# Stacked attention scores: the keys' low parts in both halves of the rows

## The chip, the cores and the metric

The kernel runs on one core of one Trainium2 chip. The metric is the device time of one execution in microseconds (us). Five engines work side by side, each in the order of its own queue: TensorE (PE in the profile; its weight loads have a row of their own, PEld), VectorE (DVE), ScalarE (ACT), GpSimd (POOL) and SyncE (SP, which issues most of the DMAs).

## The reference

Two stacks of two layers each work on 512 tokens of 1024 features in float32. A layer of the first stack projects the normalised tokens, runs three attention mixers beside each other, adds their projected results under sigmoid gates, and ends in a SwiGLU. The second stack has a retention layer and a gated linear recurrence. The change touches two of the three mixers of the first stack. Both have heads of 64 features:

```python
# dilated mixer, three groups of four heads; a group's band of keys per block of 128 queries
s = jnp.einsum('ncqhd,nckhd->nchqk', qb, kb) * (D ** -0.5)   # D = 64
s = jnp.where(mask, s, NEG_INF)                              # then softmax, then P V
# neighbourhood mixer, eight heads; each query sees 8 x 16 keys of the 8 x 64 grid
s = jnp.einsum('bchd,bcnhd->bhcn', q_row, kg) * scale + bias # then softmax, then P V
```

## The kernel before

**Precision.** TensorE reads float32r, which holds fewer bits than float32. Every operand is therefore kept as a pair: `split` (lines 267 to 274) writes the high part on ACT (`hi = round(src)`) and the low part on DVE (`lo = src - hi`). A product of two pairs is three matmuls, high x high, high x low and low x high (`mm3`, lines 283 to 285), all added into one PSUM bank.

**Stacked scores.** A head of 64 features fills half of TensorE's 128 rows. For group 0 of the dilated mixer and for the neighbourhood mixer the kernel therefore stacks the parts. A slot of the pool `R` is a tile [128, 2, 512]; the two heads of a pair (`e` = 0, 1) use its two halves of 512 columns. `stack_q` puts a query's high part into the 64 rows of its own side and the low part into the other 64. `stack_k` puts the keys' high part into both sides of one slot, and the keys' low part into the own side only of a second slot. `stacked` then needs two matmuls instead of three:

```python
SIDES = ((slice(0, 64), slice(64, 128)), (slice(64, 128), slice(0, 64)))
nc.tensor.matmul(s, lhsT=q[:, e, qsl], rhs=k[0][:, e, ksl], start=True, stop=False)       # line 750, 128 rows
nc.tensor.matmul(s, lhsT=q[own, e, qsl], rhs=k[1][own, 0, ksl], start=False, stop=True)   # line 751, 64 rows
```

The stationary operand is a block of 128 queries, the moving one the keys: 512 of them in the dilated mixer (32 calls over the two layers), 192 or 256 in the neighbourhood mixer (32 calls each). The dilated mixer's other groups (`s1`) and all other products go through `mm3` or `pv`. `pv` (lines 714 and 715) multiplies one stationary block of values, high parts and low parts beside each other, with the high and then with the low parts of the transposed softmax. The first mixer (MLA) has scores of 96 rows, through `mm3`.

**Order of the work.** The three mixers follow one another in each layer: MLA, dilated, neighbourhood. In each, `pipeline` issues the scores of a block one or two blocks ahead of the rest of it (softmax on DVE and ACT, transposes on PE by lines 903, 1051, 1056 and 1170, splits, `pv`). Between the blocks lie projections of the next pair (`chunk`, 24 matmuls of `mm3` each), among them those that end in `stack_q` and `stack_k`, and the merges of the mixer before (`fill`). Semaphores, and the order of instructions on each engine, are set when the program is built, by a planner that follows the program's order as a priority and starts what it holds to be ready. `high_priority` moves the splits of weights forward. `stack_k` runs twelve times: in each of the two layers for two pairs of heads of dilated group 0 and four pairs of the neighbourhood mixer.

Of the kernel before, what the change touches and what calls it, by code (L numbers as in the profile page):

```python
# [24 lines left out]
WPRI = 120  # how far ahead of the program's order weight splits are placed  # L25
HPRI = 400  # the same for the splits of h
LD = (3, 2)  # of every LD[0] LRU weight units, LD[1] go through R's slots
NG = 5  # tiles of the first branch's gates made before the attention
PD = (2, 2, 1)  # depth of the attention pipelines: MLA, dilated, neighbourhood
NM = (4, 2, 4, 1, 4, 2)  # per mixer: of every NM[2i] blocks, NM[2i+1] scale the softmax by the row sum on ACT  # L30


# ---------------------------------------------------------------- host layout
# Token order of the first block: (column group of 8, row, column in the group) of the 8 x 64 grid.
# [4 lines left out]
def _shape_constants():  # L39
# [13 lines left out]
    # dilated attention: position (b, i) is token NA_TOK[4 i + b]  # L53
# [32 lines left out]
def _na_bias_index():  # L86
    """For each query block: index into one head's flat rpb table, or one past it where no key is seen."""
    out = []
    n = 15 * 31
    for qb, (kb0, off, w) in enumerate(NA_Q):  # L90
        qt = NA_TOK[qb * 128:(qb + 1) * 128]
        k0 = kb0 * 128 + off if qb else 0
        kt = NA_TOK[k0:k0 + w]
        qr, qc = qt // 64, qt % 64
        kr, kc = kt // 64, kt % 64
        cs = np.clip(qc - 8, 0, 48)
        seen = (kc[None] >= cs[:, None]) & (kc[None] < cs[:, None] + 16)
        idx = (kr[None] - qr[:, None] + 7) * 31 + (kc[None] - qc[:, None] + 15)
        out.append(np.where(seen, idx, n))
    return np.concatenate(out, 1)  # L100
# [7 lines left out]
def _tiles(w):  # L108
    """[K, N] -> [N/128, 128, K/128, 128]: one output tile's weights lie together per partition."""
    k, n = w.shape  # L110
    return w.reshape(k // 128, 128, n // 128, 128).transpose(2, 1, 0, 3)


def _wide(w):
    """[K, 512] -> [K/256, 128, 2, 4, 128]: four output tiles' weights, two row tiles to a unit."""
    k, n = w.shape
    return w.reshape(k // 256, 2, 128, n // 128, 128).transpose(0, 2, 1, 3, 4)
# [21 lines left out]
def layout(inp):  # L139
# [32 lines left out]
    # [l, unit, 128, chunk, k tile, 128]  # L172
# [41 lines left out]
# ---------------------------------------------------------------- the kernel  # L214
# [12 lines left out]
def kernel(ctx: ExitStack, tc: tile.TileContext, d, out):  # L227
# [35 lines left out]
    # ---- primitives  # L263
# [3 lines left out]
    def split(src, hi, lo, scale=None):  # L267
        """src = hi + lo exactly, both on the float32r grid (scale: a number or a column)."""
        if scale is None:
            nc.scalar.copy(out=hi, in_=src)  # L270
            nc.vector.tensor_tensor(out=lo, in0=src, in1=f(hi), op=ALU.subtract)  # L271
        else:
            nc.scalar.activation(out=hi, in_=src, func=AF.Copy, scale=scale)
            nc.vector.scalar_tensor_tensor(out=lo, in0=src, scalar=scale, in1=f(hi), op0=ALU.mult, op1=ALU.subtract)
# [15 lines left out]
    def wload(src, n, keep=False):  # L290
        """A unit of weights from DRAM as a pair; kept in general slots, or in the ring until the unit after next."""
# [17 lines left out]
    def proj(ps, ap, n, rhs, keep=False):  # L309
        """ps = W^T x: W's tiles [128, n, 128] in DRAM, rhs the (hi, lo) pairs of x's n tiles.  # L310

        keep: the weights go through general slots, for more of them on their way."""
# [12 lines left out]
    def wide(pss, ap, n, rhs, ahead=(), norm=None):  # L325
        """Four output tiles at once, a row tile of x after another: for an x that is still being made.

        ahead: the first units' weights, where they are on their way; norm: x's, finished on the way."""
# [12 lines left out]
    def out_proj(first, rest, n, rhs, sink):  # L341
        """Eight output tiles, the first four of them wide."""
        pss = [MB.get() for _ in range(4)]
        wide(pss, first, n, rhs)
        for m in range(4):
            sink(m, pss[m])
            MB.put(pss[m])
        for m in range(4, 8):
            ps = MB.get()
            proj(ps, rest[m - 4], n, rhs)  # L350
            sink(m, ps)
            MB.put(ps)

    class Norm:
        """1 / sqrt(mean square over the features + eps): a column per block of tokens, and a row on all partitions."""
# [15 lines left out]
        def means(self, n, bank=None):  # L371
# [16 lines left out]
            # one Newton step, past the square root's table  # L388
# [16 lines left out]
    def warm_sqrt(dep):  # L405
        """The square root's table, loaded ahead of the norm that follows dep."""
# [7 lines left out]
    # ---- swiglu  # L414
    def ffn(h, norm, l4, later=None, between=()):
        """silu(x W1) (x W3): norm scales x where h doesn't hold that yet; later makes h's second half of the tokens."""
# [54 lines left out]
    # ---- tokens on the partitions: output projections with the norms behind them  # L471
    def half(ap, hf, nat):
        """Columns of half the tokens of a tile, with the tokens in their own order or in the first block's."""
# [4 lines left out]
    def wide_halves(pss, ap, rhs, later, nat):  # L478
        """As wide, for x's eight tiles: half of the tokens, and then (later makes them) the others."""
# [13 lines left out]
    def rstd(sm):  # L493
        """sm[:, 4] = 1 / sqrt((sm[:, 0] + sm[:, 1]) / D + eps)"""
# [16 lines left out]
    def out_tokens(src, n, act, gain, nxt, xt=None):  # L511
        """x (in FX, by blocks of tokens) += rms(y W) gain, or x = rms(xt + y W) gain; y's n tiles are act.

        nxt None: x goes out. Else it is the column of the next norm's gain: returns the next h, with its first half of
        the tokens made, and what makes the second. Ahead of a mixer the tokens go back to their own order."""
# [66 lines left out]
        def turn(hf):  # L582
            """Half the tokens of h, with the features back on the partitions."""
# [38 lines left out]
    # ---- the first block's mixers  # L622
    def first_layer(l, xsrc, h, norm, ahead=()):
# [28 lines left out]
        def merge(i, y, wname, m0, early):  # L652
            """merged += (1 + tanh(gate / 2)) (y W) for two tiles; the gate's first branch was made early, in place."""
# [25 lines left out]
        def pipeline(blocks, ahead):  # L679
            """blocks: (before, scores, rest); scores go out some blocks ahead of the rest."""  # L680
# [11 lines left out]
        def soft(pt, sm, src, negmax, ri, scalar):  # L692
            """pt = exp(src - max) / sum over the keys; the scaling on ScalarE or on VectorE."""
# [10 lines left out]
        # Values lie by (token block, head): 64 columns of the high parts and 64 of the low ones, so that a product  # L704
        # with P^T holds the two sums in the two halves of its rows.
        def value_split(ps, v, b0, nb, scale=None):
            """ps [128 tokens, nb blocks x 4 heads x 64] into blocks b0.. of v's two slots."""
# [9 lines left out]
        def pv_sum(o, rows):  # L717
            """A head's sums: the two halves of o's rows together, in the given rows."""
# [12 lines left out]
        # Queries and keys of 64 rows, of two heads: a query's high and low parts lie in the two halves of the rows,  # L731
        # against the keys' high parts twice; then its high parts against the keys' low ones.
# [8 lines left out]
        def stack_k(z):  # L741
            hi, lo = R.get(), R.get()
            for e, (own, other) in enumerate(SIDES):
                split(z[own], hi[own, e], lo[own, 0])
                nc.scalar.copy(out=hi[other, e], in_=z[own])
            return hi, lo

        def stacked(s, e, q, qsl, k, ksl):
            own = SIDES[e][0]
            nc.tensor.matmul(s, lhsT=q[:, e, qsl], rhs=k[0][:, e, ksl], start=True, stop=False)  # L750
            nc.tensor.matmul(s, lhsT=q[own, e, qsl], rhs=k[1][own, 0, ksl], start=False, stop=True)  # L751

        # ---------------- multi-head latent attention
# [183 lines left out]
        # ---------------- dilated attention, positions (b, i) = token 4 i + b of the stored order  # L937
# [7 lines left out]
        def vproj(g, order4):  # L945
            """Token-major values of four heads: [128 tokens, 4 blocks, 256] as (hi, lo) slots."""
# [148 lines left out]
        # ---------------- neighbourhood attention  # L1095
# [28 lines left out]
        def na_block(p, e, qb):  # L1124
# [36 lines left out]
            def rest():  # L1161
# [9 lines left out]
                # slot of (key block, query) in this half: key blocks hf .. hf + 2, two query blocks each  # L1171
# [10 lines left out]
                # key block, first column of its slots, first output column, width  # L1182
# [32 lines left out]
        # ---------------- output projection and residual  # L1215
# [27 lines left out]
    # ---------------- first block  # L1243
    nc.vector.memset(f(ones), 1.0)
    nc.vector.memset(epsc, EPS)
    # the tensor engine's clock rises while the first loads are on their way
# [53 lines left out]
    # ---------------- second block: x is kept with the tokens on the partitions, in the first block's order  # L1300
# [6 lines left out]
    def mixed(z, own):  # L1307
        """A mixer's output tile as a pair, with the tokens in the first block's order."""
# [7 lines left out]
    # ---------------- retention  # L1316
# [11 lines left out]
    for hd in range(4):  # L1328
# [21 lines left out]
        # values, token-major  # L1350
# [80 lines left out]
    # ---------------- gated linear recurrence  # L1431
    hp = [pair(t) for t in h]
    # cs = -8 softplus(-a) = -8 (max(-a, 0) + log1p(exp(-|a|))), log1p(e) = 2 atanh(e / (2 + e)) by its series
# [17 lines left out]
    # half the gate biases, for sigmoid(z) = (1 + tanh(z / 2)) / 2  # L1451
# [9 lines left out]
    for n in range(6):  # L1461
# [47 lines left out]
        for i in range(2):  # L1509
# [3 lines left out]
            # mult^2 = -expm1(2 log a) = T (1 + a^2), T = tanh(-log a)  # L1513
# [42 lines left out]
```

## Time and profile before

| | before |
|---|---|
| device time, median of 3 runs | 3357.36 us (3356.54 to 3357.69) |
| profiled execution, span from its first to its last instruction | 3360.7 us |
| PE busy | 3329.5 us, 99% |
| DVE busy | 1812.8 us, 54% |
| ACT busy | 1439.7 us, 43% |
| mean DMA rate | 93 GB/s |

Busy means that an instruction of the engine is in progress; the ends of matmuls are modelled, and consecutive matmuls overlap in the records. The pace of PE is therefore read from the starts: the time from one matmul's start to the next one's. For the profiled execution no time beside its span is on record; the span is 3.3 us (0.1%) above the median of the runs.

### The profile page before, as it was taken

What the parts mean: (1) busy time and instruction counts of PE and PEld (TensorE: products, weight loads), DVE (VectorE), ACT (ScalarE), POOL (GpSimd) and SP (SyncE); (2) the same over time, 40 slices, a digit from 0 to 9 for tenths busy, and PEclk for the clock granted to TensorE, in tenths of its full rate; (3) what the DMA queues carried; (4) which work ended last, traced back from release to release, by engine and by line L of the source; (5) the groups of instructions that cost most, each with busy time, mean ns of one, the idle gap of its engine ahead of it and who ended that gap; (6) DMA issues with size and microseconds to landing.
All of it is one profiled execution on the core that took longest, in us unless ns stands there. A gap on an engine that the chain in (4) does not pass through costs nothing.

```text
span 3360.7 us, 40433 instructions
## 1 busy us (share of the span) xinstructions
PE 3329.5 (99%) x15970; PEld 2798.7 (83%) x15970; DVE 1812.8 (54%) x3018; ACT 1439.7 (43%) x2321; POOL 125.3 (4%) x127
## 2 busy tenths in 40 slices
PE   9999999999999999999999999999999999999999
PEld 7898888888888898888888888888888888788887
DVE  7837765555347738765444355554433257753323
ACT  5735653432236626653332234433422247742322
POOL 0000001011000000001011000000000000000000
PEclk9999999999999999999999999999999999999999
DMA  4113323322333113223223322223133332223232
GB/s 160 52 49 97 94 75 101 114 96 94 102 121 95 51 60 105 91 67 125 94 94 110 126 76 85 85 79 113 63 97 104 107 107 94 80 84 101 94 104 90
DMA packets 97439, 313.77 MB, mean 93 GB/s; under 512 B 12000, under 2 KB 16736, under 8 KB 97248
## 3 DMA queue, kind: packets, MB, share of 16 engines
q1 hardware_dynamic: 95376, 308.33, 28.8%
q8 instruction: 125, 2.05, 0.3%
q10 hardware_dynamic: 1872, 2.85, 0.2%
q14 instruction: 66, 0.54, 0.0%
HBM read 298.55 MB, written 4.19 MB: 90 GB/s over the span
## 4 chain that ended last, share of the span: by engine, by line
PE 91%; ACT 4%; DVE 3%; DMA 1%; issue 1%; POOL 0%; DVEq 0%; ACTq 0%; SPq 0%
PE b L283 28%; PE b L285 28%; PE b L284 28%; PE b L715 1%; PE b L714 1%; PE b L751 1%; DVE wlo L271 1%; ACT r L270 1%; DVE fa L277 1%; PE b L1170 1%; PE b L903 1%; ACT whi L270 1%; DVE r L271 1%; DMA raw<-in_gu_dram 0%; PE b L750 0%
## 5 line engine op out<-in xcount | busy, mean ns | idle before, releaser
L283 PE MATMUL b<-r,whi 128*128 128x512 f32 (+1 forms) x3032 | 1168.3, 389 | 10.1 <-ACT whi L270 3.7
L284 PE MATMUL b<-r,whi 128*128 128x512 f32 (+1 forms) x3032 | 1170.6, 387 | 0.0
L285 PE MATMUL b<-r,wlo 128*128 128x512 f32 (+1 forms) x3032 | 1161.5, 387 | 0.0
L270 ACT CAST whi<-raw 128x1024 fp32r<-128x1024 f32 (+2 forms) x486 | 506.7, 1043 | 1231.2 <-PE b L284 696.3
L271 DVE TENSOR_TENSOR wlo<-raw,whi 128x1024 fp32r<-128x1024 f32 (+2 forms) x486 | 632.8, 1302 | 635.9 <-ACT whi L270 628.8
L283 PEld LDWEIGHTS b<-r,whi 128*128 128x128 f32 x3032 | 567.6, 188 | 126.4 <-ACT whi L270 5.5
L285 PEld LDWEIGHTS b<-r,wlo 128*128 128x128 f32 x3032 | 570.5, 188 | 114.1 <-issue 1.0
L284 PEld LDWEIGHTS b<-r,whi 128*128 128x128 f32 x3032 | 571.1, 188 | 111.2 <-issue 0.5
L284 PE MATMUL b<-wlo,r 128*128 128x512 f32 (+1 forms) x1040 | 393.6, 378 | 0.5 <-DVE wlo L271 0.5
L285 PE MATMUL b<-whi,r 128*128 128x512 f32 (+1 forms) x1040 | 393.3, 378 | 0.0
L283 PE MATMUL b<-whi,r 128*128 128x512 f32 (+1 forms) x1040 | 322.4, 377 | 1.4 <-ACT whi L270 1.4
L283 PEld LDWEIGHTS b<-whi,r 128*128 128x128 f32 x1040 | 222.3, 214 | 30.4 <-ACT whi L270 2.3
L284 PEld LDWEIGHTS b<-wlo,r 128*128 128x128 f32 x1040 | 222.4, 214 | 30.1 <-issue 1.0
L285 PEld LDWEIGHTS b<-whi,r 128*128 128x128 f32 x1040 | 222.5, 214 | 29.0 <-issue 1.0
L283 PE MATMUL b<-r,r 128*128 128x512 f32 (+4 forms) x640 | 226.8, 357 | 6.2 <-ACT p L694 5.4
L284 PE MATMUL b<-r,r 128*128 128x512 f32 (+4 forms) x640 | 225.2, 353 | 0.1
L285 PE MATMUL b<-r,r 128*128 128x512 f32 (+4 forms) x640 | 223.9, 352 | 0.0
L277 DVE TENSOR_TENSOR fm<-b,fa 128x512 f32<-128x512 f32 x120 | 82.7, 691 | 238.8 <-PE b L285 238.7
L270 ACT CAST r<-b 128x512 fp32r<-128x512 f32 (+3 forms) x264 | 125.8, 495 | 117.3 <-PE b L1170 29.4
L277 DVE TENSOR_TENSOR fa<-fa,fa 128x512 f32<-128x512 f32 x202 | 135.6, 696 | 63.3 <-ACT fa L1392 29.0
L271 DVE TENSOR_TENSOR r<-b,r 128x512 fp32r<-128x512 f32 (+3 forms) x264 | 147.1, 570 | 37.7 <-ACT r L270 36.7
L277 DVE TENSOR_TENSOR fm<-b,fm 128x512 f32<-128x512 f32 (+2 forms) x86 | 59.1, 687 | 175.9 <-PE b L285 135.3
(167 smaller groups left out, 2937.3 us busy)
## 6 DMA issues: line engine op xcount, KB each, us to landing
raw<-in_gu_dram SPq DMA_DIRECT2D x176, 512.0 KB, 3.5
raw<-in_w_in_dram SPq DMA_DIRECT2D x96, 512.0 KB, 3.6
raw<-in_f_out_dram SPq DMA_DIRECT2D x44, 512.0 KB, 3.5
raw<-in_r_in_dram SPq DMA_DIRECT2D x32, 512.0 KB, 3.5
raw<-in_l_in_dram SPq DMA_DIRECT2D x24, 512.0 KB, 3.5
raw<-in_w_tok_dram SPq DMA_DIRECT2D x22, 512.0 KB, 3.5
raw<-in_w_v_dram SPq DMA_DIRECT2D x20, 512.0 KB, 3.9
raw<-in_r_v_dram SPq DMA_DIRECT2D x16, 512.0 KB, 3.9
```

The source lines that it names most:

```text
L270: nc.scalar.copy(out=hi, in_=src)
L271: nc.vector.tensor_tensor(out=lo, in0=src, in1=f(hi), op=ALU.subtract)
L277: nc.vector.tensor_tensor(out=out_, in0=a, in1=b, op=op)
L283: nc.tensor.matmul(ps, lhsT=l[0], rhs=r[0], start=start, stop=False)
L284: nc.tensor.matmul(ps, lhsT=l[0], rhs=r[1], start=False, stop=False)
L285: nc.tensor.matmul(ps, lhsT=l[1], rhs=r[0], start=False, stop=stop)
L714: nc.tensor.matmul(o, lhsT=lt, rhs=ph, start=start, stop=False)
L715: nc.tensor.matmul(o, lhsT=lt, rhs=pl, start=False, stop=stop)
L751: nc.tensor.matmul(s, lhsT=q[own, e, qsl], rhs=k[1][own, 0, ksl], start=False, stop=True)
L903: nc.tensor.transpose(tp[:, k * 128:k * 128 + 128], b["p"][:, k * 128:k * 128 + 128], ident)
L1170: nc.tensor.transpose(t0[:, k * 128:k * 128 + 128], pt[:, k * 128:k * 128 + 128], ident)
```

## The change

Three lines of code are edited, and comments and docstrings are replaced by empty lines or dropped, with the line numbers kept (one line more in `stack_k`, one less in `stacked`; the two matmuls stay lines 750 and 751). The keys' low part of head `e` now lies in half `e` of the slot's columns (before, both heads' low parts lay in half 0, in different rows), and an ACT copy puts it into the other 64 rows as well. The second matmul takes all 128 rows of the stacked queries, the same stationary operand as the first. It so adds low x low to the scores, which before were left out. No slot is added: the second slot of `stack_k` was a whole tile before.

```diff
         def stack_k(z):
             hi, lo = R.get(), R.get()
             for e, (own, other) in enumerate(SIDES):
-                split(z[own], hi[own, e], lo[own, 0])
+                split(z[own], hi[own, e], lo[own, e])
                 nc.scalar.copy(out=hi[other, e], in_=z[own])
+                nc.scalar.copy(out=lo[other, e], in_=f(lo[own, e]))
             return hi, lo

         def stacked(s, e, q, qsl, k, ksl):
-            own = SIDES[e][0]
             nc.tensor.matmul(s, lhsT=q[:, e, qsl], rhs=k[0][:, e, ksl], start=True, stop=False)
-            nc.tensor.matmul(s, lhsT=q[own, e, qsl], rhs=k[1][own, 0, ksl], start=False, stop=True)
+            nc.tensor.matmul(s, lhsT=q[:, e, qsl], rhs=k[1][:, e, ksl], start=False, stop=True)
```

## Rows read from the trace of the kernel before

**Rows 1.** The page: busy time by engine, and the chain that ended last.

```profile
PE 3329.5 (99%) x15970; PEld 2798.7 (83%) x15970; DVE 1812.8 (54%) x3018; ACT 1439.7 (43%) x2321; POOL 125.3 (4%) x127
...
PE 91%; ACT 4%; DVE 3%; DMA 1%; issue 1%; POOL 0%; DVEq 0%; ACTq 0%; SPq 0%
```

**Rows 2.** PE's waits, 248 to 530 us: total, times, longest (us).

```profile
PE b L750 <- DVE sm L1153: 0.6, 1, 0.6
```

**Rows 3.** Line 751, whole run: duration ns min/median/max, first and last start, shapes.

```profile
L751 PE MATMUL b<-r,r x96: 351/381/502, 248.4 to 1490.4; 64*128 64x512 f32 x32, 64*128 64x256 f32 x32, 64*128 64x192 f32 x32
```

**Rows 4.** Timeline of PE, first dilated block: start us, duration us.

```profile
247.85 0.39 PE L285 MATMUL b<-r,wlo 128*128 128x512 f32 x1
248.08 0.39 PE L750 MATMUL b<-r,r 128*128 128x512 f32 x1
248.40 0.50 PE L751 MATMUL b<-r,r 64*128 64x512 f32 x1
248.83 0.38 PE L283 MATMUL b<-r,r 128*128 128x256 f32 x1
249.05 0.28 PE L284 MATMUL b<-r,r 128*128 128x256 f32 x1
```

**Rows 5.** Timeline of the weight loads there, idle time in brackets.

```profile
248.40 0.18 PEld L751 LDWEIGHTS b<-r,r 64*128 64x128 f32 x1 [0.35 <-issue]
248.82 0.19 PEld L283 LDWEIGHTS b<-r,r 128*128 128x128 f32 x1 [0.25 <-issue]
```

**Rows 6.** Timeline of PE, neighbourhood blocks of 192 and of 256 keys.

```profile
388.39 0.25 PE L750 MATMUL b<-r,r 128*128 128x192 f32 x1
388.58 0.35 PE L751 MATMUL b<-r,r 64*128 64x192 f32 x1
388.86 0.50 PE L285 MATMUL b<-r,wlo 128*128 128x512 f32 x1
389.20 0.40 PE L283 MATMUL b<-r,whi 128*128 128x512 f32 x1
...
389.89 0.28 PE L750 MATMUL b<-r,r 128*128 128x256 f32 x1
390.09 0.38 PE L751 MATMUL b<-r,r 64*128 64x256 f32 x1
390.40 0.39 PE L715 MATMUL b<-r,r 128*128 128x256 f32 x1
390.63 0.28 PE L714 MATMUL b<-r,r 128*128 128x256 f32 x1
390.74 0.27 PE L715 MATMUL b<-r,r 128*128 128x256 f32 x1
```

**Rows 7.** Timeline of PE, MLA scores of 96 rows.

```profile
146.41 0.40 PE L283 MATMUL b<-r,r 96*128 96x512 f32 x1
146.64 0.40 PE L284 MATMUL b<-r,r 96*128 96x512 f32 x1
146.88 0.39 PE L285 MATMUL b<-r,r 96*128 96x512 f32 x1
```

**Rows 8.** Line 745, the copies of the keys' high parts, whole run.

```profile
L745 ACT CAST r<-fa x24: 617/618/621, 166.1 to 1453.1; 64x512 fp32r<-64x512 f32 x24
```

**Rows 9.** Busy time in the first layer's dilated and neighbourhood stretches.

```profile
248.00:380.00 132.00, 132.00 (x720) 109.01 (x719) 97.43 (x212) 70.34 (x118) 4.56 (x11) 1.00 0.31 93
380.00:530.00 150.00, 149.35 (x786) 122.99 (x785) 101.13 (x262) 86.58 (x187) 10.95 (x11) 1.00 0.27 84
```

Columns: window and length, then busy us of PE, PEld, DVE, ACT and POOL (instructions), PE clock, DMA share, GB/s.

**Rows 10.** Timeline of ACT, the last `stack_k` of layer one.

```profile
475.93 0.62 ACT L745 CAST r<-fa 64x512 fp32r<-64x512 f32 x1
...
477.21 0.62 ACT L745 CAST r<-fa 64x512 fp32r<-64x512 f32 x1
```

**Rows 11.** Timeline of DVE, its last low part.

```profile
477.22 0.69 DVE L271 TENSOR_TENSOR r<-fa,r 64x512 fp32r<-64x512 f32 x1 [0.60 <-ACT r L270]
```

**Rows 12.** Timeline of PE, the first use of these keys.

```profile
483.36 0.25 PE L750 MATMUL b<-r,r 128*128 128x192 f32 x1
```

## The prediction

> **What bounds the kernel.** I read the page first. PE is busy for 99% of the span and 91% of the chain that ended last is PE's own work [rows 1]. The next question is whether the two stages that the change touches are the same, so I looked at PE's waits there. In the first layer's dilated and neighbourhood stretches, 248 to 530 us, the profile names one wait, of 0.6 us [rows 2], and PE shows as busy for all but 0.65 of the 282 us [rows 9]. So a microsecond that PE gains in this stretch is a microsecond of the end, as long as the softmax keeps up, and one that another engine loses costs nothing until PE waits for it.
>
> "Busy" says little about pace, since the ends of matmuls are modelled. So I went to the timeline and read starts. A product of 512 columns is followed by the next after 0.23 us (line 285 to line 750, 247.85 to 248.08) [rows 4], one of 256 columns after 0.11 us (line 714 to 715, 390.63 to 390.74) [rows 6]; half of 0.23 would be 0.115, and I use 0.12. Around the 64-row product it is otherwise. In the dilated block, line 750 to 751 takes 0.32, line 751 to the next 0.43, and that next one, which has 256 columns, 0.22 [rows 4]. The weight loads tell why: elsewhere the next load starts while the matmul before it streams, but the load for line 751 starts only at 248.40, with its own matmul and after 0.35 us of idle, and the load behind it again only at 248.82, with its matmul, after 0.25 us of idle; both times nothing is named as waited for ("issue") [rows 5]. PE empties on the way into the 64-row product and again on the way out, and on the way out the load of the next weights is not hidden.
>
> **The change, part by part.** *The second matmul, 96 times [rows 3].* It becomes a copy of the first in shape: 128 rows, the same stationary block, the same number of columns. What it will cost is on show in the trace already: `pv` multiplies one stationary block of 128 rows twice in a row into one bank, at 0.11 us for 256 columns [rows 6]. So I price the stacked pair at the undisturbed pace and count what the switch costs now, over three intervals, from the start of line 750 to the start of the second product after line 751.
>
> - 512 keys: 248.08 to 249.05 is 0.97 us [rows 4]. Undisturbed, 0.23 + 0.23 + 0.12 (the last has 256 columns) = 0.58. Lost: 0.39.
> - 192 keys: 388.39 to 389.20 is 0.81 [rows 6]. The third product has 512 columns, 0.23. The first two have no undisturbed row of their own; they lie between 192/512 of 0.23 = 0.09 and the 0.12 of 256 columns. That gives 0.41 to 0.47, lost 0.34 to 0.40. I take 0.38, near the proportional end, as 256 columns are close to half of 512.
> - 256 keys: 389.89 to 390.63 is 0.74 [rows 6]. Undisturbed, 3 x 0.12 = 0.36. Lost: 0.38.
>
> The loss hardly depends on the width, which suits a fixed price per switch. Of each width there are 32 [rows 3]: 32 x (0.39 + 0.38 + 0.38) = 36.8 us, say 37. With the ends of the 192-key price it is 35.5 to 37.5. The sum assumes that the 96 places are like these three.
>
> *The streaming itself.* The product has twice the rows but the same columns. Scores of 96 rows go at 0.23 to 0.24 us per 512 columns [rows 7], as those of 128 rows do, so rows that are used cost nothing. Here a rule of the Trainium skill speaks against the change. Its page "TensorE: Matmul & The Clock Gate", section "Why this matters for your kernels", says that a single matmul of 32 rows takes as long as one of 128. By that rule, taken for 64 rows, the second product would have nothing to give back, and the gain would be 0 instead of 37 us (rival B). The trace agrees for the streaming of 96 rows and disagrees around the 64-row products, where three intervals together are 0.38 us too long.
>
> *Where the low part lies* (half `e` instead of half 0): the same DVE instruction to another address, nothing.
>
> *24 new copies on ACT.* The nearest row is its twin, the copy of the high part: same shape, 0.618 us [rows 8]. That makes 24 x 0.618 = 14.8 us more of ACT, 7.4 per layer, and no DMA. It is covered by ACT's idle time: 156.9 busy of 282 us in this stretch [rows 9]. Without the cover it costs its 14.8 us. But each copy reads what DVE has just written, so it adds a wait too: ACT stands until the low part is done (0.69 us [rows 11]) and then copies. Queued behind it on ACT are the softmax's exponentials and scalings and the splits of weights and of the transposed softmax, and PE waits for those. Are the keys themselves late? The tightest place I found is the last pair: ACT's last copy starts at 477.21 and DVE's low part ends at 477.91 [rows 10, 11]; two more copies and a wait make that about 479.5, and the first scores of the pair start at 483.36 [rows 12]. So no. What is left is the delay of other work on ACT. Its bounds are 0 (all within slack) and 14.8 us (PE waits through each copy). The row nearest to it is the 0.6 us of waiting in the stretch [rows 2], near 0. PE will run some 6.5% faster there (18.5 of 282 us), so the softmax has less time. I take 1 us per layer, 2 in all.
>
> *The planner.* With 24 more instructions it may order others anew. I can't price this; I put it within the 2 us and the range.
>
> **Sum.** Against the profiled span: 3360.7 - 37 + 2 = 3325.7 us. The runs' median is 3.3 us below that span, and I carry the difference over: 3357.4 - 35 = 3322 us, 1.0% faster.
>
> **Rivals.**
>
> *A. The gain is given back in the softmax.* PE reaches the transposes earlier and ACT comes later, so PE waits for ACT. For it: the new copies wait for DVE, and DVE is the busier helper, 198.6 of 282 us [rows 9]. Against it: one wait of 0.6 us today. With 5 to 14.8 us lost, the time is 3325 to 3337.
>
> *B. No gain.* The stall belongs to the place and not to the 64 rows (say, to the second product into one bank), so that the number of rows changes nothing. It would then stay, or reappear in another interval: 3357 plus 0 to 15 us. Against it: `pv`, which is the new shape, has no such stall, and line 750 itself starts on time after another 128-row product [rows 4]. The Trainium skill's rule above ("TensorE: Matmul & The Clock Gate", "Why this matters for your kernels") would lead here.
>
> *C. Slower.* The new copy blocks ACT's queue behind DVE, and PE stands for every one. To eat 37 us, each of the 24 must cost PE 1.54 us. One copy and the one low part that it reads are 0.62 + 0.69 = 1.31, which is not enough (31 us, still 6 faster); with one more DVE instruction of 0.69 in front it is 2.0, 48 us in all, and the time 3357 - 37 + 48 = 3368. Against it: it needs the wait at nearly all 24, while PE has another 128-row product to run at most places.
>
> **How the numbers follow.** The forecast (gain 35.5 to 37.5, loss under 5) gets 0.72: 3320 to 3327. A gets 0.16, B 0.06, C 0.06. About 0.2%, 6.7 us, is what a measurement of this kernel can tell from no change. Faster by more: the forecast and A, 0.88. Within: B with a small cost, 0.05. Slower: C, and B with a large cost, 0.07. The range takes the forecast and nearly all of A: its upper end is a gain of 35.5 with 14.8 lost, 3337; its lower end is the gain of 37.5 and no loss, 3320, less 2 us since the 96 places were priced by three.
>
> **What would show it.** Right: line 751 appears with 128 rows, starts 0.23, 0.12 and about 0.09 us after line 750 for 512, 256 and 192 keys, and the product behind it starts as soon; the weight loads there have no idle time; 24 new ACT copies of 0.62 us lie in `stack_k`; and the first layer's stretch from 248 to 530 us is some 17.5 us shorter. Wrong: the intervals shrink but PE's waits for ACT or DVE in these stretches grow from 0.6 us to many (A, C), or the idle time before the weight loads remains at 128 rows (B). The forecast would also fail if the 93 places that I don't show were mostly overlapped by other stalls, so that there was less to gain.

## The result, and the profile after

The changed kernel takes 3323.65 us (median of 4 runs, 3323.01 to 3325.1) against 3356.95 us before (median of 4, 3356.41 to 3357.69): 33.3 us less, a ratio of 0.990 with a 95% interval of 0.9886 to 0.9914. The prediction said 3322, with a range of 3318 to 3337.

The first view is again the page of the changed kernel, busy time by engine and the chain that ended last; it answers to [rows 1].

```profile
PE 3290.6 (99%) x15970; PEld 2791.7 (84%) x15970; DVE 1812.7 (55%) x3018; ACT 1454.0 (44%) x2345; POOL 124.3 (4%) x127
...
PE 90%; DVE 4%; ACT 4%; DMA 1%; issue 1%; DVEq 0%; SPq 0%; ACTq 0%
```

ACT has 24 instructions and 14.3 us more, PE the same number of instructions and 38.9 us less, and PE still sets the end. The second view is PE's timeline at the first dilated block and at two neighbourhood blocks, where [rows 4, 6] stood. The weight loads follow, at the first of them, where [rows 5] stood, and at the second.

```profile
246.25 0.39 PE L750 MATMUL b<-r,r 128*128 128x512 f32 x1
246.48 0.39 PE L751 MATMUL b<-r,r 128*128 128x512 f32 x1
246.71 0.28 PE L283 MATMUL b<-r,r 128*128 128x256 f32 x1
246.82 0.28 PE L284 MATMUL b<-r,r 128*128 128x256 f32 x1
...
380.62 0.25 PE L750 MATMUL b<-r,r 128*128 128x192 f32 x1
380.71 0.28 PE L751 MATMUL b<-r,r 128*128 128x192 f32 x1
380.83 0.41 PE L285 MATMUL b<-r,wlo 128*128 128x512 f32 x1
381.08 0.39 PE L283 MATMUL b<-r,whi 128*128 128x512 f32 x1
...
381.77 0.28 PE L750 MATMUL b<-r,r 128*128 128x256 f32 x1
381.89 0.27 PE L751 MATMUL b<-r,r 128*128 128x256 f32 x1
382.00 0.28 PE L715 MATMUL b<-r,r 128*128 128x256 f32 x1
382.12 0.28 PE L714 MATMUL b<-r,r 128*128 128x256 f32 x1
```

```profile
246.26 0.19 PEld L751 LDWEIGHTS b<-r,r 128*128 128x128 f32 x1
246.48 0.19 PEld L283 LDWEIGHTS b<-r,r 128*128 128x128 f32 x1
...
380.63 0.19 PEld L751 LDWEIGHTS b<-r,r 128*128 128x128 f32 x1
380.74 0.19 PEld L285 LDWEIGHTS b<-r,wlo 128*128 128x128 f32 x1
380.85 0.19 PEld L283 LDWEIGHTS b<-r,whi 128*128 128x128 f32 x1
```

At the dilated block the load for line 751 starts with line 750's matmul, 0.22 us ahead of its own, and the next one as early; no idle time is noted. The three intervals from the start of line 750 take 0.57 us with 512 keys (before 0.97), 0.46 with 192 (0.81) and 0.35 with 256 (0.74): 0.40, 0.35 and 0.39 us less.

The saving lies where the 96 products lie. By the view of line 750, its first and last starts were 248.1 and 1490.2 us before and are 246.3 and 1455.2 now (first row before, second after):

```profile
L750 PE MATMUL b<-r,r x96: 248/334/481, 248.1 to 1490.2; 128*128 128x512 f32 x32, 128*128 128x256 f32 x32, 128*128 128x192 f32 x32
L750 PE MATMUL b<-r,r x96: 247/334/477, 246.3 to 1455.2; 128*128 128x512 f32 x32, 128*128 128x256 f32 x32, 128*128 128x192 f32 x32
```

From first to last that is 1242.1 us before and 1208.9 after, 33.2 less, as much as the difference of the medians (33.3). In the first layer alone line 750 runs from 248.08 to 514.27 us before and from 246.25 to 495.93 after, 16.5 us less.

The profiled spans differ by more, 39.2 us (3360.7 and 3321.5). The other 6.0 lie outside the stacked scores, and most of them are the clock and not the change. In the profiled execution of before, TensorE's granted clock fell from its full level (2.4 GHz) to half (1.2 GHz) three times between the first loads and the end, each time behind a wait of PE (1.7, 1.3 and 1.9 us). The three stretches, with the mean granted clock as the third number from the end:

```profile
138.00:146.00 8.00, 6.72 (x30) 5.87 (x31) 7.81 (x15) 6.18 (x13) 0.00 (x0) 0.79 0.35 104
2745.00:2755.00 10.00, 8.29 (x53) 7.69 (x52) 9.41 (x28) 7.24 (x23) 0.00 (x0) 0.83 0.26 93
2864.00:2874.00 10.00, 8.06 (x29) 6.15 (x28) 7.36 (x13) 6.16 (x10) 0.00 (x0) 0.83 0.16 52
```

That is a loss of 0.21 of 8 us and twice 0.17 of 10 us, 5.1 us in all. In the profiled execution of after the clock stays at 1.00 from 20 to 3310 us, although PE has waits of much the same length (1.7, 1.2 and 2.0 us). One of the three falls lies ahead of the stacked scores and two behind them, so the 33.2 us are free of them.

### The profile page after: what moved, and what is told of

It reads as the page before. It is cut to its first block, busy times and chain, and to the rows that moved or that the text cites. A ratio compares the mean times of both kernels' runs of the same rounds, so it can differ in the third digit from the quotient of the medians.

```text
span 3321.5 us, 40467 instructions
## 1 busy us (share of the span) xinstructions
PE 3290.6 (99%) x15970; PEld 2791.7 (84%) x15970; DVE 1812.7 (55%) x3018; ACT 1454.0 (44%) x2345; POOL 124.3 (4%) x127
## 4 chain that ended last, share of the span: by engine, by line
PE 90%; DVE 4%; ACT 4%; DMA 1%; issue 1%; DVEq 0%; SPq 0%; ACTq 0%
PE b L283 28%; PE b L285 28%; PE b L284 28%; PE b L715 1%; PE b L714 1%; ACT r L270 1%; DVE wlo L271 1%; DVE r L271 1%; DVE fa L277 1%; ACT whi L270 1%; PE b L1170 1%; DMA raw<-in_l_in_dram 1%; PE b L903 1%; DMA raw<-in_gu_dram 0%; ACT fa L508 0%
```

## The experiments

Nine runs follow, one of them the changed kernel once more; the medians of before were 3359.2 to 3359.8 us beside them, and each ratio is to the kernel before on the same chip. The edits are cut to the lines that matter. Where an edit adds or drops lines, line 750 and its neighbours have other numbers.

**The rows alone, without the copies.** Against the changed kernel:

```diff
-                nc.scalar.copy(out=lo[other, e], in_=f(lo[own, e]))
-            nc.tensor.matmul(s, lhsT=q[:, e, qsl], rhs=k[1][:, e, ksl], start=False, stop=True)
+            nc.tensor.matmul(s, lhsT=q[:, e, qsl], rhs=k[0][:, e, ksl], start=False, stop=True)
```

> The second product takes all 128 rows, but against the keys' high parts once more, and the 24 ACT copies are gone; the keys' low parts are left out of the stacked scores. Theory 1 (the 64-row product costs PE about 0.38 us each time it comes between 128-row products, 37 us in all, and the copies give back some 3 of them): 3320 us, 3 to 4 below the changed kernel. Rival (the copies cost nothing, and the price of a switch is 0.35): the same as the changed kernel within 1 us, 3323 to 3325.

Measured: 3324.77 us, ratio 0.9898 (0.9884 to 0.9911), 34.4 us less than before. The changed kernel is 33.3 less in its first measurement and 33.8 in the run that repeats it. So the medians give the copies about 1 us, which can't be told from nothing. The traces give them less: from the first to the last start of a stacked block's first product (line 749 in this build, 247.0 to 1456.1) it is 1209.1 us without the copies and 1208.9 with them. Theory 1's 3320 did not come, and the rival is nearer: without any copy the 128 rows give 34.4 and not 37.

**The copies alone.** Against the kernel before:

```diff
-                split(z[own], hi[own, e], lo[own, 0])
+                split(z[own], hi[own, e], lo[own, e])
...
+                nc.scalar.copy(out=lo[other, e], in_=f(lo[own, e]))
...
-            nc.tensor.matmul(s, lhsT=q[own, e, qsl], rhs=k[1][own, 0, ksl], start=False, stop=True)
+            nc.tensor.matmul(s, lhsT=q[own, e, qsl], rhs=k[1][own, e, ksl], start=False, stop=True)
```

> The 24 copies are made, but the second product still takes the 64 rows of its own side, so nobody reads the copies. Theory 1 (copies cost some 3 us, most of them in the shorter time that a faster PE leaves): 3357 to 3360. Rival C of the prediction (PE waits through each copy): 3357 + 15 = 3372 or more. Copies free: 3357 within 1 us.

Measured: 3360.2 us, ratio 1.0002 (0.9993 to 1.0011), so between 2.4 us less and 3.7 us more. The copies take their 0.62 us each on ACT:

```profile
L746 ACT CAST r<-r x24: 617/619/621, 168.7 to 1454.7; 64x512 fp32r<-64x512 f32 x24
```

That is 14.8 us of ACT, of which PE loses at most 3.7. Rival C, which needed 37 us, is out, and so is its smaller form, 15 us. From the first to the last start of line 750 (246.9 to 1489.7) the trace has 1242.8 us, 0.7 more than before.

**Two products of 64 rows, one behind the other.** Against the kernel before:

```diff
-            nc.tensor.matmul(s, lhsT=q[own, e, qsl], rhs=k[1][own, 0, ksl], start=False, stop=True)
+            n = (ksl.stop - ksl.start) // 2
+            for i in range(2):
+                nc.tensor.matmul(s[:, i * n:i * n + n], lhsT=q[own, e, qsl], rhs=k[1][own, 0, ksl.start + i * n:ksl.start + i * n + n],
+                                 start=False, stop=i == 1)
```

> The kernel before, with the second product cut into two products of half the keys each, both of 64 rows, one behind the other: 192 products of 64 rows in place of 96, the same columns. Theory 1 (the price is for changing between 128 and 64 rows): hardly more than the issue of 96 products, 3357 to 3363. Rival (each product of 64 rows costs its 0.38 us): another 37 us, 3394.

Measured: 3373.11 us, ratio 1.0044 (1.0031 to 1.0056), 10 to 19 us more. Neither number came. In the timeline of PE, with 512 keys and with 192 (rows of two products together are marked x2):

```profile
248.00 0.39 PE L750 MATMUL b<-r,r 128*128 128x512 f32 x1
248.31 0.50 PE L753 MATMUL b<-r,r 64*128 64x256 f32 x2
248.74 0.39 PE L283 MATMUL b<-r,r 128*128 128x256 f32 x1
248.97 0.39 PE L283 MATMUL b<-r,whi 128*128 128x512 f32 x1
...
386.40 0.25 PE L750 MATMUL b<-r,r 128*128 128x192 f32 x1
386.58 0.42 PE L753 MATMUL b<-r,r 64*128 64x96 f32 x2
386.93 0.50 PE L283 MATMUL b<-r,whi 128*128 128x512 f32 x1
387.27 0.39 PE L284 MATMUL b<-r,whi 128*128 128x512 f32 x1
```

With 512 keys the three intervals, now with one product more, take 0.97 us, exactly as before: the second product of 64 rows costs nothing of its own. With 192 keys they take 0.87 against 0.81, 0.06 more. The rival's 0.38 per product is out. But the order of PE's other work changed too in this build: by the records PE goes from 128 rows into 64 not 96 times but 109 times, since other products came between some of the halves. An estimate from these rows: 13 more ways in and out at 0.38 are 5 us, and 0.06 at the 64 narrow places 4 more. From the first to the last start of line 750 (248.0 to 1496.6) the trace has 6.5 us more than before. Where the rest of the 14 arises stays open. The next pair of kernels was made to avoid that.

**Once or twice through the same rows.** Both products are cut into halves of the keys, and only the order of the four differs. All other products on PE, and the instructions of DVE, ACT and GpSimd, come in the same order in both traces. The first line of the edit is the loop in groups, the second the one in turns (the comments are added here):

```diff
-            for i, low in ((0, 0), (1, 0), (0, 1), (1, 1)):   # 128, 128, 64, 64 rows
+            for i, low in ((0, 0), (0, 1), (1, 0), (1, 1)):   # 128, 64, 128, 64 rows
                 sl = slice(ksl.start + i * n, ksl.start + i * n + n)
                 if low:
                     nc.tensor.matmul(s[:, i * n:i * n + n], lhsT=q[own, e, qsl], rhs=k[1][own, 0, sl], start=False, stop=i == 1)
                 else:
                     nc.tensor.matmul(s[:, i * n:i * n + n], lhsT=q[:, e, qsl], rhs=k[0][:, e, sl], start=i == 0, stop=False)
```

> The kernel before, with both products of a stacked pair cut into halves of the keys, in the order 128, 128, 64, 64 rows: one way into the 64 rows and one out, as before, with 192 more products. It is the partner of the next run. Theory (price per change of rows): about that of the run with two products of 64 rows, 3373, plus the loads of 96 more products of 128 rows that narrow ones can't hide, up to 5 us: 3373 to 3380.

> The same four products in the order 128, 64, 128, 64 rows: two ways in and two out at each of the 96 places, and nothing else changed. Theory (0.34 to 0.39 us for a way in and out): 33 to 37 us above the run before it. Rival (the loss belongs to the 64-row product as such, by its number): the same time as the run before it.

Measured: 3374.74 us (1.0047, 1.003 to 1.0064) in groups and 3401.39 us (1.0127, 1.0112 to 1.0142) in turns, 26.7 us between them. The number of 64-row products is the same, so the rival's 0 is out; the theory's 33 to 37 is too high. In the timelines of PE, first in groups, then in turns:

```profile
247.62 0.40 PE L756 MATMUL b<-r,r 128*128 128x256 f32 x2
247.95 0.50 PE L754 MATMUL b<-r,r 64*128 64x256 f32 x2
248.38 0.50 PE L283 MATMUL b<-r,whi 128*128 128x512 f32 x1
248.72 0.40 PE L284 MATMUL b<-r,whi 128*128 128x512 f32 x1
...
385.96 0.32 PE L756 MATMUL b<-r,r 128*128 128x96 f32 x2
386.21 0.42 PE L754 MATMUL b<-r,r 64*128 64x96 f32 x2
386.56 0.50 PE L283 MATMUL b<-r,whi 128*128 128x512 f32 x1
386.89 0.39 PE L284 MATMUL b<-r,whi 128*128 128x512 f32 x1
```

```profile
247.96 0.28 PE L756 MATMUL b<-r,r 128*128 128x256 f32 x1
248.17 0.38 PE L754 MATMUL b<-r,r 64*128 64x256 f32 x1
248.48 0.38 PE L756 MATMUL b<-r,r 128*128 128x256 f32 x1
248.80 0.38 PE L754 MATMUL b<-r,r 64*128 64x256 f32 x1
249.11 0.50 PE L283 MATMUL b<-r,whi 128*128 128x512 f32 x1
249.44 0.40 PE L284 MATMUL b<-r,whi 128*128 128x512 f32 x1
...
392.38 0.21 PE L756 MATMUL b<-r,r 128*128 128x96 f32 x1
392.52 0.31 PE L754 MATMUL b<-r,r 64*128 64x96 f32 x1
392.76 0.31 PE L756 MATMUL b<-r,r 128*128 128x96 f32 x1
393.00 0.31 PE L754 MATMUL b<-r,r 64*128 64x96 f32 x1
393.24 0.50 PE L283 MATMUL b<-r,whi 128*128 128x512 f32 x1
393.58 0.39 PE L284 MATMUL b<-r,whi 128*128 128x512 f32 x1
```

With 512 keys, from the first of the four to the second product behind them: 1.10 us in groups, 1.48 in turns. One more way in and out costs 0.38 us, the price of the prediction. With 192 keys it is 0.93 and 1.20, only 0.27; my reading is that pairs of such narrow products wait for weight loads in groups too. And the number of ways in is not what the expectation took. By the records PE goes into 64 rows 108 times in groups and 191 times in turns, 83 more and not 96, as other products lie between some of the halves in both. The 26.7 us are 0.32 for each of the 83, between the two prices shown.

**One mixer at a time.** `stacked` and `stack_k` got a flag, set for the dilated or for the neighbourhood mixer alone; the other keeps its 64 rows. Of the edit, against the kernel before:

```diff
-            own = SIDES[e][0]
+            own = slice(0, 128) if wide_lo else SIDES[e][0]
```

> The change for dilated group 0 alone (512 keys, 32 of the 96 products, 8 of the 24 copies); the neighbourhood mixer keeps its 64 rows. Theory 1 (a fixed price per change of rows, whatever the width): a third of the 33.3 us, 3346. Rival (the loss grows with the columns; 512 of every 960 are here): 53% of it, 3339.

> The complement of the run with the dilated mixer alone: the 64 products of 192 and 256 keys take 128 rows (16 of the 24 copies), the 32 of 512 keys keep 64. Theory (a fixed price per change of rows, two thirds of the places; for 192 keys a little less, since the changed trace shows that a product that narrow can't hide the weight load behind it): 21 to 23 us below the kernel before. Rival (the loss grows with the columns, 47% of them here): 16 below.

Measured: 3348.93 us for the dilated mixer, ratio 0.9968 (0.9956 to 0.998), 7 to 15 us less; 3339.88 for the neighbourhood, 0.9941 (0.9927 to 0.9954), 15 to 25 less. The first excludes the rival's 18 us and holds the theory's 11. The second holds both 16 and 21 to 23 and doesn't tell them apart. By their medians the two give 10.3 and 19.6 us, 29.9 in all, 3 to 4 below the whole change, within their intervals.

**The copies by DMA.** Against the changed kernel, which ran again beside it:

```diff
-                nc.scalar.copy(out=hi[other, e], in_=z[own])
-                nc.scalar.copy(out=lo[other, e], in_=f(lo[own, e]))
+                nc.sync.dma_start(out=f(hi[other, e]), in_=f(hi[own, e]))
+                nc.sync.dma_start(out=f(lo[other, e]), in_=f(lo[own, e]))
```

> The changed kernel once more, as the partner on this chip: 33.3 us below the kernel before, 0.990 of it.

> The changed kernel, with the copies of the high and of the low parts into the other rows made by DMAs on SyncE's queue: 48 copies, 29.6 us, less on ACT, and 48 DMAs that SyncE's queue waits with. Theory (ACT's copies are off the path but for some 1 us): the same as the changed kernel within 2 us. Rival (ACT's copies cost several us): 3 or more below it. Third way (SyncE's queue stands behind the wait for the keys, and weights come late): above it.

Measured: 3325.94 us (0.9901, 0.9886 to 0.9915) for the changed kernel and 3324.2 (0.9897, 0.9883 to 0.9912) with DMAs. The intervals cover each other. Taking 48 copies off ACT gives nothing that shows, which says once more that PE doesn't lose time to these copies; it is not a version that beats the changed kernel.

## Why the prediction was right

**The mechanism.** It said that PE empties on the way into and out of a 64-row product, and that 128 rows end that. The weight loads after the change and the two orders of the same four products show it: 0.38 us for one more way in and out with 512 keys, with everything else alike. In all runs the product and its weight load change their rows together, so which of the two PE empties for is not shown. After the change, the Trainium skill's page "TensorEngine Tiling (Array Packing)", under "Key Properties", fits: it says that a change of the tiling mode, not of the tile alone, drains the engine. By that rule, what counts is the number of changes and not that of 64-row products, and the trace agrees (0.97 us for one as for two of them in a row with 512 keys). That a product of 64 rows runs in a tiling mode of its own no trace here shows. The rule set against the change, that few rows take as long as many ("TensorE: Matmul & The Clock Gate", "Why this matters for your kernels"), isn't wrong for this: it speaks of a matmul by itself, and the price here is paid where it meets its neighbours.

**The sum.** The three prices were 0.39, 0.38 and 0.38 us; the trace after gives 0.40, 0.35 and 0.39. The 192-key one was taken near the wrong end of its bounds (0.34 to 0.40): the new product of 192 columns starts in time, 0.09 us after line 750, but the one behind it comes 0.12 us later and its own successor 0.25, as the weight loads there start 0.11 us apart (380.63, 380.74, 380.85). The prediction had the product behind start as soon, which it did not. That makes 32 x (0.40 + 0.35 + 0.39) = 36.5 us where 36.8 was said.

The three places were to stand for 96, and the traces can settle that. I took, around every line 751, the intervals into it, out of it and behind it, each less the usual interval of a product of its width. Before, every one of the 96 places loses at least 0.33 us; none is covered by another stall. The sum over all of them is about 38 us before, and about 4 remain after, most of these at 192 keys. So the gain is about 34 us where the prediction said 37.

**What was given back.** The forecast allowed 2 us, for the copies and the softmax's shorter time. Of about 34 us gained 33.2 are left from the first to the last stacked block, and the one wait of PE that grew there, by 1.1 us, accounts for the difference. It lies at the second neighbourhood block of each layer: line 750 stands until DVE has worked through the scores before it (line 1153). It grew from 0.6 us [rows 2] to 1.2. The view of PE's waits after the change, first layer, 246 to 496 us:

```profile
PE b L750 <- DVE sm L1153: 1.2, 1, 1.2
```

Over both layers this wait is 1.3 us before, 2.0 with 128 rows alone, 2.2 with the copies alone, 2.4 with both, and 1.1 with the copies by DMA. So it is rival A at one place, but neither the faster PE nor the copies alone are its cause, and 1.1 us is all that it takes. The forecast's two terms were both too large, 37 for 34 and 2 for 1; they cancel in part, and that 3322 came within 2 us of the measured time owes something to this.

**The keys in time.** The last pair of layer one was expected to be ready about 2 us after its old end and well before its use. ACT's timeline after:

```profile
463.53 0.62 ACT L746 CAST r<-r 64x512 fp32r<-64x512 f32 x1
464.18 0.75 ACT L270 CAST r<-b 128x384 fp32r<-128x384 f32 x2
464.96 0.62 ACT L746 CAST r<-r 64x512 fp32r<-64x512 f32 x1
```

ACT didn't stand for DVE: the planner put the second copy behind two splits of the softmax, and it ends at 465.58, while the pair's first scores start at 467.60, 2.0 us later. The slack was 5.5 us before (477.91 to 483.36). I would expect it to fail next if ACT or DVE got more work there; no run tried that.

**The chances.** A came at 1.1 us of the 5 that it began with, B and C did not come. The planner did reorder PE's work, at no price that can be told from the rest. In the run with two 64-row products its order cost 13 more ways in and out, and about a third of the 14 us stays unexplained.

## What to carry to other kernels

Where TensorE is the bound, look at the starts around matmuls that use half of the rows: a lone one of 64 rows between full ones cost 0.35 to 0.40 us here at 192 to 512 columns, in intervals that a view of busy time shows as work. If the idle rows can be filled, do it, and pay with an engine that has slack; a useful term and mere copies were tried here, zeros were not. If they can't, put such matmuls behind one another, so that the way in and out is paid once, and count in the trace whether they stayed together.

## What the runs showed of the hardware

- The price has three parts. With 512 keys they are 0.09 us before the 64-row product starts (0.32 instead of 0.23), 0.20 before the next one starts (0.43), and 0.10 behind that (0.22 instead of 0.12), although the records call PE busy throughout.
- Scores of 96 rows, in the same kernel, pay none of it: among themselves [rows 7], and also where they meet 128 rows (0.23 us on the way in, from 146.18 to 146.41, and 0.22 on the way out, from 146.88 to 147.10). The 64-row product is not alone, though: the few products of 32 rows (line 762, eight in the whole run) show the same intervals, 0.32 us into them behind 512 columns (38.93 to 39.25) and 0.33 behind the product that follows them (39.84 to 40.17); no run tried these by themselves.
- Weight loads of 0.19 us follow one another at 0.11 us, so a product of 256 columns (0.12) hides its successor's load, and one of 192 (0.09) doesn't quite.
